# Attention's chunks in one list with a fixed order per engine, sums of x moved into the retention, loads of made products asked for ahead

## The chip, the cores and the metric

The kernel runs on one core of one Trainium2 chip. The metric is the device time of one execution in microseconds (us), given as the median of several runs. The core has five engines that run their own instruction streams in order: TensorE (PE, matmuls and transposes; its weight loads are listed apart as PEld), VectorE (DVE), ScalarE (ACT), GpSimd (POOL) and SyncE (SP), which here issues nearly all DMAs.

## The reference

One encoder layer. 16 learned meta tokens are put in front of x (1024 rows of 1024), so there are 1040 positions.

```
u = rms_norm(h, pre_w)
z = u @ w_in                       # 7680 columns
rq, rk, rv, rg, aq, ak, av, ag, gr, ga = split(z)
# branch A: 4 heads of bidirectional retention in chunks of 128, with decays
o_r = group_norm(retention_forward + retention_backward) * ret_nw * silu(rg)
# branch B: 8 query heads in 2 groups, windowed softmax attention, a sink logit, the meta keys always visible
s = rotary(aq) . rotary(ak) * scale + mask        # 128 queries, up to 384 + 16 keys
m = max(max(s), sink);  p = exp(s - m)
o_a = (p / (sum(p) + exp(sink - m))) @ v * silu(ag)
mix = sigmoid(gr) * (o_r @ w_rb) + sigmoid(ga) * (o_a @ w_ab)
out = h + rms_norm(mix @ w_out, post_w)
```

## The kernel before

All matmuls are in split float32: each operand is a high part h and a low part l in the fast format, and `mm3` (L69) adds three matmuls hh, lh, hl (lines L71, L72, L73) into one PSUM tile. High parts are made on ScalarE or GpSimd (`pool_hi`, L75), low parts on VectorE by subtraction (`dve_lo`, L78).

The work goes through these stages:

- **Start** (to about 46 us): x is loaded, split into `big`, and the queries and keys of retention head 0 are projected.
- **Retention** (`retention`, L434; to about 349 us). For each head h: a forward loop over c = 0..8, in which `stage1(c + 1)` projects a chunk of V (`pv`), splits it (L465, L466) and makes the decayed keys and scores, and `stage2(c)` forms the inner and cross products (`pa`) and the state (`pkv`); then a backward loop with `pb`, the group norm and transposes (`to`).
- **Attention** (`attention`, L1207; about 349 to 616 us). Called for four pairs of heads hp, each with 8 chunks n of 128 queries for two heads e_. `stage1(n)` makes the scores of both heads (`ps`, three matmuls each), the row minimum on VectorE (L1254), the exponential with its sum on ScalarE (L1257), the reciprocal (L1260) and the scaling on GpSimd (L1266). `stage2(n)` transposes the probabilities on PE (`pt`, L1276 to L1283) and splits them: pah and pal for the first two blocks of keys, pm for the meta keys, pbh and pbl for the third block. `stage3(n)` multiplies them with the values (`po`, seven or ten matmuls), copies the result to `oa` (L1312) and stores it every second chunk.
- **Gates and output projections** (`Phase`, `run`; from about 598 us): 16 pairs of weight blocks for the gates (`bz`), two branch projections and the output projection, by a seven-product scheme whose operands are sums and differences of quarter blocks.

Between the dependent steps of retention and attention stands independent work, the **filler**. `filler` (L604) joins generators; `fill(n)` advances them by n units. A unit of `gen_qk` (next retention head), `gen_ak` (attention keys) or `gen_aq` (attention queries, `paq`) is one step of the inner dimension, three matmuls; 8 units make one PSUM tile, which `rope_evac` (L158) rotates with three VectorE operations and one GpSimd addition. `gen_pre(u)` (L701) makes one or two of the gates' seven products ahead of their stage (**made products**, `pe`, 4 units each): it loads raw weights (`we`), forms a combination in three VectorE subtractions or additions (L711 to L713), splits it and stores the products to `e_d`. `FILL` (L26) says how many units follow each chunk of attention. The lists are `fills(hp)` (L1346).

`sum_row(k)` (L666) makes four rows of differences of x's quarter blocks for the later stage: two loads, two scalings on ScalarE (L672), four subtractions on VectorE (L676), four stores to `xs_d` (L677). It is called in attention, for hp 1 and 2 after chunks 2 and 5.

All raw weights, and the rows of `sum_row`, go through two SBUF buffers of 512 KB with the tag `wr`; the split weights through four buffers `wh` and four `wl`. A load can be issued when its buffer's last reader is done.

The order of every engine's instructions is set at build time: the tile context is opened with `schedule_with_timeline_sim=True`, and its planner orders the traced instructions by its own estimate of times, earlier traced ones first where several are ready. `with tc.issue_after(i):` puts each instruction of the block that runs on the engine of i behind i. Attention before has one such edge in its loop, which keeps the filler behind the third score product before the latest pair:

```
with tc.issue_after(scored[-5]) if len(scored) > 4 else ExitStack():
    fill(FILL[hp][n])
```

So what PE does between the scores, transposes and value products of neighbouring chunks is the planner's choice. `x_to_out` (L1340) copies most of x to out, DRAM to DRAM, behind the first store of attention.

Of the kernel before, what the change touches and what calls it, by code (L numbers as in the profile page):

```python
# [25 lines left out]
FILL = (6, 5, 5, 5, 5, 5, 5, 4), (6,) * 8, (6, 5, 5, 4, 4, 4, 4, 0), (7, 7, 7, 7, 6, 6, 8)  # L26
# [12 lines left out]
def block_kernel(ctx: ExitStack, tc: tile.TileContext, xT, x, w_in, w_rb, w_ab, w_out, vecs, dec, sink,  # L39
# [28 lines left out]

    def mm3(o, ah, al, bh, bl, first, last, free_group=False):  # L69
        kw = {"skip_group_check": True} if free_group else {}  # L70
        nc.tensor.matmul(o, ah, bh, start=first, stop=False, **kw)  # L71
        nc.tensor.matmul(o, al, bh, start=False, stop=False, **kw)  # L72
        return nc.tensor.matmul(o, ah, bl, start=False, stop=last, **kw).ins  # L73
# [360 lines left out]
    def retention(h, fill):  # L434
# [194 lines left out]

    def gen_aq(hp, i):  # L630
        if not i:
            wq[hp] = load_w(w_in, U_AQ + hp)
            aq[hp] = {}
        a, b = HALVES[i]
        for e_ in range(2):
# [3 lines left out]
            aq[hp][e_, i] = o  # L639
            yield  # L640
# [3 lines left out]

    def gen_ak(g):
        if not wak:
            wak.append(load_w(w_in, U_AK))
# [17 lines left out]

    def sum_row(k):  # L666

        x = {}
        for i in range(2):
            t = keep.tile([P, 4, 256], F32, tag="wr", bufs=2, name=f"xs{i}{k}").rearrange("p a b -> p (a b)")  # L670
            nc.sync.dma_start(t, xT[4 * i + k, :, NM:T])
# [3 lines left out]
        for n, o, a, b in SUMS:  # L675
            nc.vector.tensor_tensor(x[o], x[a], x[b], ALU.subtract)  # L676
            nc.sync.dma_start(xs_d[n][k], x[o])  # L677

# [22 lines left out]
    def gen_pre(u):  # L701

        g = nc.vector.tensor_tensor
        n = P * len(PRE[u])
        raw = [keep.tile([P, 4, 256], F32, tag="wr", bufs=2, name=f"we{u}_{j}") for j in range(len(PRE[u]))]
        for j, t in enumerate(reversed(raw)):
            nc.sync.dma_start(t[:, :, 0:n], w_in[gates[u], :, 4 - 4 * j:8 - 4 * j, 0:n])
        t = raw[-1]
        if n > P:
            v = t[:, :, P:n]  # L710
            g(v, raw[0][:, :, P:n], v, ALU.add)  # L711
            g(v, v, raw[0][:, :, 0:P], ALU.subtract)
            g(v, t[:, :, 0:P], v, ALU.subtract)  # L713
        h = wp.tile([P, 4, 256], R, tag="wh", bufs=4, name=f"weh{u}")[:, :, 0:n]
        l = wp.tile([P, 4, 256], R, tag="wl", bufs=4, name=f"wel{u}")[:, :, 0:n]
        nc.scalar.copy(h, t[:, :, 0:n])
        dve_lo(l, t[:, :, 0:n], h)
        for p in PRE[u]:
# [9 lines left out]
            nc.sync.dma_start(e_d[u, p], o)  # L728
            yield
# [10 lines left out]
    pre = all_pre()  # L740
# [449 lines left out]
    def gen_av():  # L1190
        w = load_w(w_in, U_AV)
        for c in range(9):
# [9 lines left out]
            if c % 2 == 0:  # L1202
                yield

    scored, softmax, stored, values = [], [], [], {}

    def attention(hp, fill):  # L1207
        g = hp // 2
        kh, kl = kT[g]
# [257 lines left out]
```

## Time and profile before

| what | value |
|---|---|
| median of 3 runs | 1107.57 us (1107.34 to 1107.73) |
| profiled execution | 1106.49 us, span from first to last instruction 1104.7 us |
| mean granted TensorE clock | 0.994 |
| attention, stretch 349.1 to 592 us | PE busy 227.08 of 242.90 us |
| largest wait of PE by one releaser | ps behind nm (L1254): 11.6 us in 16 waits |

A row of the groups reads: line, engine, operation, output <- inputs by the program's names, shapes, count, then busy time in us and mean ns of one, then the idle time of the engine before them and what ended it. "Busy" of PE includes modelled ends of pipelined matmuls, so two neighbours overlap: a matmul of 512 columns is shown as 0.39 us and the next starts 0.23 us after it. A row of the stretches reads: start:end, length, then busy time and number of instructions of PE, PEld, DVE, ACT, POOL, then the granted clock, the DMA engines' busy share and GB/s.

### The profile page before, as it was taken

How to read it: one execution, taken by the hardware profiler on the slowest of the kernel's cores; microseconds unless marked ns; L12 is line 12 of the kernel's file. 1: busy time of each engine (PE TensorE's matmuls, PEld its weight loads, DVE VectorE, ACT ScalarE, POOL GpSimd, SP SyncE). 2: the span in 40 equal slices, each digit the busy share in tenths (PEclk: the TensorE clock that was granted, in tenths of full speed). 3: DMA queues.
4: the chain of work that ended last, by engine and by line, in shares of the span. 5: the costliest groups of instructions: out<-in, count | busy, mean ns of one | idle time of the engine just before them, and what ended most of it. 6: DMA issues, size and time to landing. Idle time of an engine off the chain costs nothing.

```text
span 1104.7 us, 17067 instructions
## 1 busy us (share of the span) xinstructions
PE 1067.4 (97%) x5939; PEld 916.4 (83%) x5939; DVE 875.6 (79%) x1797; ACT 504.1 (46%) x1126; POOL 219.8 (20%) x276
## 2 busy tenths in 40 slices
PE   8999999999999989998998999999999999999997
PEld 7898999988989867986787788788888888787886
DVE  7897778868976866788646899999789889866765
ACT  7141432513414534645356744545456545433442
POOL 3234225143332423333220000000000000010032
PEclk9999999999999999999999999999999999999999
DMA  7121102122122545333224857899963765779463
GB/s 285 39 68 57 52 27 68 58 62 83 49 96 77 182 144 180 126 105 115 79 90 157 276 196 272 303 349 349 365 204 121 231 210 176 233 200 326 142 115 77
DMA packets 82902, 175.16 MB, mean 159 GB/s; under 512 B 8784, under 2 KB 22608, under 8 KB 82000
## 3 DMA queue, kind: packets, MB, share of 16 engines
q1 hardware_dynamic: 78928, 167.51, 44.5%
q0 software_dynamic: 3456, 6.29, 3.7%
q8 instruction: 46, 0.75, 0.3%
q14 instruction: 40, 0.33, 0.1%
q10 hardware_dynamic: 432, 0.28, 0.1%
HBM read 119.52 MB, written 57.67 MB: 160 GB/s over the span
## 4 chain that ended last, share of the span: by engine, by line
PE 73%; DVE 10%; DMA 9%; ACT 3%; issue 3%; POOL 1%; SPq 0%; DVEq 0%; POOLq 0%; ACTq 0%
PE bz L71 6%; PE bz L72 6%; PE bz L73 6%; PE pv L71 3%; PE pv L72 2%; PE pv L73 2%; PE br L72 2%; PE br L71 2%; PE br L73 2%; PE bo L72 2%; PE bo L71 2%; PE bo L73 2%; DMA we<-in_w_in_dram 2%; PE ba L72 2%; PE ba L73 2%
## 5 line engine op out<-in xcount | busy, mean ns | idle before, releaser
L1105 POOL DMA_DIRECT2D mx_d<-c1a x4 | 3.7, 917 | 400.8 <-DVE c1a L1096 400.8
L71 PE MATMUL bz<-T,lhz 128*128 128x512 f32 x192 | 75.6, 395 | 1.1 <-ACT u2z L887 1.1
L72 PE MATMUL bz<-T,llz 128*128 128x512 f32 x192 | 75.7, 394 | 0.0
L73 PE MATMUL bz<-T,lhz 128*128 128x512 f32 x192 | 75.6, 395 | 0.0
L71 PE MATMUL pv<-wh,big 128*128 128x256 f32 x256 | 73.9, 289 | 1.2 <-DVE m_qk L164 1.2
L72 PE MATMUL pv<-wh,big 128*128 128x256 f32 x256 | 73.7, 288 | 0.0
L73 PE MATMUL pv<-wl,big 128*128 128x256 f32 x256 | 73.4, 287 | 0.0
L72 PE MATMUL bz<-big,llz 128*128 128x512 f32 x176 | 69.6, 395 | 0.0
L73 PE MATMUL bz<-big,lhz 128*128 128x512 f32 x176 | 69.3, 394 | 0.0
L71 PE MATMUL bz<-big,lhz 128*128 128x512 f32 x176 | 69.3, 398 | 0.0
L1254 DVE CUSTOM_DVE_ANT_0 raw<-ps,mask,nsink 128x400 f32<-128x400 f32 (+1 forms) x64 | 37.9, 595 | 28.8 <-ACT p L1257 28.1
L1266 POOL TENSOR_SCALAR p<-p,den 128x400 f32<-128x400 f32 (+1 forms) x60 | 40.7, 692 | 94.2 <-DVE den L1260 72.1
L71 PE MATMUL paq<-big,wh 128*128 128x512 f32 x128 | 51.2, 400 | 0.0
L73 PE MATMUL paq<-big,wh 128*128 128x512 f32 x128 | 51.1, 399 | 0.0
L72 PE MATMUL paq<-big,wl 128*128 128x512 f32 x128 | 51.0, 398 | 0.0
L71 PEld LDWEIGHTS pv<-wh,big 128*128 128x128 f32 x256 | 49.0, 192 | 1.7 <-DVE m_qk L164 1.5
L72 PEld LDWEIGHTS pv<-wh,big 128*128 128x128 f32 x256 | 49.0, 191 | 0.2
L73 PEld LDWEIGHTS pv<-wl,big 128*128 128x128 f32 x256 | 49.0, 191 | 0.0
L1257 ACT ACTIVATE p<-raw,nm 128x401 f32<-128x401 f32 (+1 forms) x64 | 38.8, 607 | 16.7 <-PE pt L1283 6.4
L71 PEld LDWEIGHTS bz<-T,lhz 128*128 128x128 f32 x192 | 36.2, 188 | 10.3 <-ACT u2z L887 1.9
L73 PEld LDWEIGHTS bz<-T,lhz 128*128 128x128 f32 x192 | 36.2, 188 | 8.4
L72 PEld LDWEIGHTS bz<-T,llz 128*128 128x128 f32 x192 | 36.2, 188 | 8.4
(631 smaller groups left out, 3633.6 us busy)
## 6 DMA issues: line engine op xcount, KB each, us to landing
wrz<-in_w_in_dram SPq DMA_DIRECT2D x32, 512.0 KB, 6.0
wr<-in_w_in_dram SPq DMA_DIRECT2D x29, 512.0 KB, 3.7
e<-e SPq DMA_DIRECT2D x40, 256.0 KB, 3.9
we<-in_w_in_dram SPq DMA_DIRECT2D x16, 512.0 KB, 3.8
tg<-tg_d SPq DMA_DIRECT2D x32, 256.0 KB, 5.0
T<-preT SPq DMA_DIRECT2D x6, 1024.0 KB, 8.6
oTr_d<-ost SPq DMA_DIRECT2D x16, 256.0 KB, 2.1
xs<-in_xT_dram SPq DMA_DIRECT2D x8, 512.0 KB, 3.4
```

What stands on the lines that cost most here:

```text
L71: nc.tensor.matmul(o, ah, bh, start=first, stop=False, **kw)
L72: nc.tensor.matmul(o, al, bh, start=False, stop=False, **kw)
L73: return nc.tensor.matmul(o, ah, bl, start=False, stop=last, **kw).ins
L1105: nc.gpsimd.dma_start(d, to, accum_op=ALU.add)
L1254: nc.vector.tensor_tensor_reduce(raw[e_][:, 1:1 + wid], s[:, 0:wid], mask[:, mo:mo + wid], -SCALE, nsink[:, hd:hd + 1], ALU.add, ALU.min, ...
L1257: nc.scalar.activation(p[:, 0:1 + wid], raw[e_][:, 0:1 + wid], AF.Exp, scale=-1.0, bias=nm_[:, e_:e_ + 1], accum_out=den[:, e_:e_ + 1])
L1266: nc.gpsimd.tensor_scalar(pt[e_][:, 0:wid], pt[e_][:, 0:wid], den[:, e_:e_ + 1], 1.0, op0=ALU.mult, op1=ALU.mult)
```

## The change

Five things are changed.

1. The four calls of `attention(hp, fill)` become one generator over a list of 32 chunks (hp, n). The first chunk of the next pair is thereby traced ahead of the last chunk of the pair before, except for (2, 0), whose keys belong to the second group.
2. A helper `follow` puts a block behind several instructions. `latest` holds the last matmul or transpose traced. In the loop, PE's order is fixed: scores of the next chunk, transposes of this one, filler, value products of this one. ScalarE and VectorE parts of the next scores stand behind the last `oa` copy and the last low part (`lo`); those of the transposes stand behind the last exponential (`exp`) and reciprocal (`sum`). The last two chunks are left to the planner, as before.
3. The projection of attention's V (`gen_av`) stops before its last block; that block comes behind the scores of chunk (0, 0). The low and high parts of the attention queries are made when the tile is rotated, except for pair 0's first half.
4. `sum_row` is split: `sum_fetch(h)` issues the loads at step c = 1 of retention head h, and the scalings, subtractions and stores run at c = 3, behind that step's split of V. Attention has none of it.
5. Weights of attention's filler are loaded from hooks at given units of the generators ahead of their use, and `gen_pre` is split into `pre_fetch` (loads), `pre_parts` (combination and split, behind the last reciprocal) and the products. The filler amounts are distributed anew; one made product (8 units) moves from pair 1 to pair 2, and half of the second group's keys (16 units) to the end of pair 1. The total is the same.

```diff
-FILL = (6, 5, 5, 5, 5, 5, 5, 4), (6,) * 8, (6, 5, 5, 4, 4, 4, 4, 0), (7, 7, 7, 7, 6, 6, 8)
+FILL = (6, 5, 5, 5, 5, 5, 4, 5), (6, 5, 5, 6, 6, 6, 6, 16), (6, 5, 5, 5, 5, 5, 4, 5), (7, 7, 7, 7, 6, 6, 8)
...
+    def follow(*ins):
+        st = ExitStack()
+        for i in ins:
+            st.enter_context(tc.issue_after(i))
+        return st
...
@@ retention, loop over c
             if c == 1:
                 while pend:
                     pend.pop(0)()
+                sum_fetch(h)
+            if c == 3:
+                with follow(state["v"], state["vl"]):
+                    sum_row(h)
...
@@ gen_aq
         if not i:
-            wq[hp] = load_w(w_in, U_AQ + hp)
+            if hp not in wq:
+                load_aq(hp)
...
             aq[hp][e_, i] = o
+            if hp or i:
+                split_q(hp, e_, i)
             yield
...
+    def pre_fetch(u):
         n = P * len(PRE[u])
         raw = [keep.tile([P, 4, 256], F32, tag="wr", bufs=2, name=f"we{u}_{j}") for j in range(len(PRE[u]))]
         for j, t in enumerate(reversed(raw)):
             nc.sync.dma_start(t[:, :, 0:n], w_in[gates[u], :, 4 - 4 * j:8 - 4 * j, 0:n])
+        fetched_w[u] = raw
+    def pre_parts(u):
+        raw, n = fetched_w.pop(u), P * len(PRE[u])
         t = raw[-1]
+        with follow(*softmax[-1:]):
...
+    def gen_pre(u):
+        if u not in parts:
+            pre_fetch(u)
+            pre_parts(u)
+        h, l = parts.pop(u)
+        ahead = 9 < u < 13
+        if ahead:
+            pre_fetch(u + 1)
         for p in PRE[u]:
...
+            if ahead and p == 2:
+                pre_parts(u + 1)
             yield
...
@@ attention
-        stage1(0)
-        for n in range(NB):
-            if n < NB - 1:
-                stage1(n + 1)
...
-            stage2(n)
-            if hp < 3 or n < NB - 2:
-                with tc.issue_after(scored[-5]) if len(scored) > 4 else ExitStack():
-                    fill(FILL[hp][n])
-            if hp in (1, 2) and n in (2, 5):
-                sum_row(2 * hp - 2 + n // 3)
...
-            stage3(n)
+        chunks = [(hp, n) for hp in range(4) for n in range(NB)]
+        fill = filler(fills(0))[0]
+        av = gen_av()
+        next(av)
+        stage1(0, 0)
+        with follow(*latest):
+            next(av, None)
+        for (hp, n), follows in zip(chunks, chunks[1:] + [None]):
+            if follows and follows != (2, 0):
+                with follow(*latest, *marks("oa", "lo")):
+                    stage1(*follows)
...
+            with follow(*latest, *marks("exp", "sum")) if (hp, n) < (3, NB - 2) else ExitStack():
+                stage2(hp, n)
+            if (hp, n) < (3, NB - 2):
+                if (hp, n) == (1, NB - 1):
+                    fill = filler(fills(2))[0]
+                with follow(*latest):
                     fill(FILL[hp][n])
...
+            with follow(*latest) if (hp, n) < (3, NB - 2) else ExitStack():
+                stage3(hp, n)
+            if follows == (2, 0):
+                with follow(*latest, *marks("oa", "lo")):
+                    stage1(2, 0)
+                with follow(*latest):
+                    fill(2 * KT)
...
     def fills(hp):
-        l = [gen_aq(hp, 1), pieces(pre, (8, 16, 0, 32)[hp])]
-        if hp == 2:
-            l.insert(0, gen_ak(1))
-        if hp < 3:
-            l.append(gen_aq(hp + 1, 0))
-        return l
+        if hp == 1:
+            return [hooked(gen_aq(1, 1), {5: [(pre_fetch, 8)], 11: [(pre_parts, 8)], 15: [(load_aq, 2)]}), pieces(pre, 8),
+                    hooked(gen_aq(2, 0), {5: [(load_ak,)]})]
+        if hp == 3:
+            return [hooked(gen_aq(3, 1), {3: [(pre_fetch, 10)], 9: [(pre_parts, 10)]}), pre]
+        return [*([gen_ak(1)] if hp else []), hooked(gen_aq(hp, 1), {5: [(load_aq, hp + 1)]}),
+                hooked(gen_aq(hp + 1, 0), {3: [(pre_fetch, 7 + hp)], 9: [(pre_parts, 7 + hp)]}), pieces(pre, 8)]
```

More of the change, by code (lines that the diff above doesn't have):

```diff
@@ L72, in mm3 @@
         nc.tensor.matmul(o, al, bh, start=False, stop=False, **kw)
-        return nc.tensor.matmul(o, ah, bl, start=False, stop=last, **kw).ins
+        latest[:] = [nc.tensor.matmul(o, ah, bl, start=False, stop=last, **kw).ins]
+        return latest[0]
+    def follow(*ins):
[3 more added lines that the diff above has]
+        return st
     def pool_hi(o, i):
@@ L738, in all_pre @@
             yield from gen_pre(u)
-    pre = all_pre()
+    pre, fetched_w, parts = all_pre(), {}, {}
+    scored, softmax, stored, values = [], [], [], {}
     with tc.issue_after(normed):
@@ L1201, in gen_av, with attention, vsplit @@
                 nc.scalar.activation(vraw[:, c - 1], t[:, 0:256], AF.Copy, scale=rcol[:, c:c + 1])
-            if c % 2 == 0:
+            if c == NB - 1:
                 yield
[L1205 to L1209, printed above, removed]
-        kh, kl = (t.rearrange("p a b -> p (a b)") for t in (kh, kl))
-        vs = values.setdefault(g, {})
+    def attention():
         oa, raw = [None], {}
         st1, st2 = {}, {}
-        def vsplit(b):
+        def vsplit(hp, b):
+            g = hp // 2
             a_ = ap.tile([P, P], R, tag="vh", bufs=NB, name=f"vh{hp}_{b}")
@@ L1311, in stage3 @@
             o0 = P * (n % 2)
[L1312 removed]
+            last["oa"] = nc.scalar.copy(oa[0][:, :, o0:o0 + P],
+                                        po[:, 0:256].rearrange("p (e t) -> p e t", e=2)).ins
             if n % 2:
```

116 lines of the change are left out of this document (65 added, 51 removed).

## The prediction

> **What bounds the kernel now.** I read the page first, then the busy time by stretches, then the groups of the stretch that the change rewrites, then single moments of it.
>
> ```profile
> span 1104.7 us, 17067 instructions
> PE 1067.4 (97%) x5939; PEld 916.4 (83%) x5939; DVE 875.6 (79%) x1797; ACT 504.1 (46%) x1126; POOL 219.8 (20%) x276
> ```
>
> TensorE (PE) is busy in 97% of the span, so an edit pays only where PE waits. The stretches tell where that is (columns: PE, weight loads, VectorE, ScalarE, GpSimd busy with their instructions, then clock, DMA share, GB/s).
>
> ```profile
> 103.00:245.00 142.00, 142.00 (x1069) 134.56 (x1068) 113.23 (x289) 49.78 (x149) 47.73 (x69) 1.00 0.17 56
> 245.00:319.50 74.50, 71.97 (x523) 66.84 (x522) 62.16 (x158) 24.74 (x75) 25.87 (x34) 1.00 0.27 90
> 319.50:349.10 29.60, 29.14 (x246) 28.63 (x245) 19.52 (x58) 9.61 (x26) 9.40 (x16) 1.00 0.08 28
> 349.10:592.00 242.90, 227.08 (x1281) 193.53 (x1279) 168.99 (x392) 125.34 (x333) 74.18 (x86) 0.99 0.38 124
> 440.00:500.00 60.00, 60.00 (x380) 54.40 (x379) 45.88 (x109) 32.32 (x90) 21.94 (x25) 1.00 0.39 126
> 592.00:616.00 24.00, 21.73 (x107) 17.78 (x108) 20.26 (x37) 17.20 (x40) 0.00 (x0) 0.93 0.74 251
> 640.00:660.00 20.00, 20.00 (x88) 16.20 (x87) 19.15 (x33) 11.68 (x21) 0.00 (x0) 1.00 0.61 193
> ```
>
> Attention, 349.1 to 592, has 15.8 us without PE work (242.90 - 227.08). The retention before it has almost none until head 3 (245 to 319.5: 2.5 us), and the projection of V beside the end of head 3 (319.5 to 349.1) 0.5. Busy hides more, since a matmul's modelled end reaches past the next one's start. So I count the work of attention instead.
>
> ```profile
> L71 PE MATMUL paq<-big,wh 128*128 128x512 f32 x112 | 44.9, 401 | 0.0
> L71 PE MATMUL pe<-big,weh 128*128 128x512 f32 x56 | 22.1, 394 | 0.0
> L71 PE MATMUL ps<-kTh,aqh 128*128 128x400 f32 x48 | 18.5, 386 | 7.1 <-DVE nm L1254 7.1
> L71 PE MATMUL po<-pah,vh 128*128 128x256 f32 x58 | 17.6, 303 | 2.0 <-ACT oa L1312 2.0
> ```
>
> Each row stands for one of the three matmuls of a product. So 3 x (112 + 56) = 504 of the 1281 have 512 columns, 144 have 400, and 633 have 128 to 272. The spacing of 512 columns is 20.00 / 88 = 0.227 us (row 640:660). For the others I use 0.18 and, between the 0.11 of a transpose and the 0.125 of 272 columns, 0.117. That makes 114 + 26 + 74 = 214 us of work in 242.9: **about 28 us of attention is not work.** One such place:
>
> ```profile
> 392.01 0.28 PE L72 MATMUL po<-pah,vl 128*128 128x256 f32 x1
> 392.13 0.28 PE L73 MATMUL po<-pal,vh 128*128 128x256 f32 x1
> 393.34 0.39 PE L71 MATMUL po<-pbh,vh 128*128 128x256 f32 x1 [0.55 <-ACT pbh L1298]
> 395.23 0.49 PE L71 MATMUL ps<-kTh,aqh 128*128 128x272 f32 x1 [1.39 <-DVE nm L1254]
> 395.97 0.63 PE L71 MATMUL paq<-big,wh 128*128 128x512 f32 x1
> 396.39 0.63 PE L72 MATMUL paq<-big,wl 128*128 128x512 f32 x1
> ```
>
> The scores (ps) and the value products (po) of neighbouring chunks stand beside each other with no filler (paq) between. Each waits for a softmax or split only just started, and the filler comes when nothing waits. Between 440 and 500 the filler lies between them and PE has no idle time at all: the same chunk, better ordered, is free of waits.
>
> The rows at 395.97 and 396.39 start 0.42 us apart where warm ones start 0.227 apart: after waits of 0.55 and 1.39 us PE runs at about half rate. [...]
>
> **The change, part by part.** *Fixed order in the chunk loop.* PE's order becomes scores of chunk n+1 (S), transposes of n (T), filler, value products of n (O). PE works on S for 6 x 0.18 = 1.1 us, on T for 8 x 0.11 = 0.9, on 5 filler units for 15 x 0.227 = 3.4, on O for 10 x 0.117 = 1.2: 6.6 us. The chains that must fit:
>
> ```profile
> L1254 DVE CUSTOM_DVE_ANT_0 raw<-ps,mask,nsink 128x400 f32<-128x400 f32 x48 | 30.0, 629 | 17.7 <-ACT p L1257 17.1 <-PE ps L73 0.3
> L1257 ACT ACTIVATE p<-raw,nm 128x401 f32<-128x401 f32 x48 | 30.4, 633 | 9.8 <-PE pt L1279 3.8 <-PE pt L1283 2.7 <-DVE nm L1254 2.6
> L1257 ACT ACTIVATION_READ_ACCUMULATOR p<-raw,nm 128x1 f32 x64 | 12.1, 188 | 0.0
> L1266 POOL TENSOR_SCALAR p<-p,den 128x400 f32<-128x400 f32 x46 | 32.2, 714 | 76.6 <-DVE den L1260 54.6 <-PE pt L1279 15.0 <-PE pt L1276 6.4
> L1286 ACT CAST pah<-pt 128x512 fp32r<-128x512 f32 x32 | 18.5, 577 | 8.8 <-PE pt L1276 8.7
> L79 DVE TENSOR_TENSOR pal<-pt,pah 128x512 fp32r<-128x512 f32 x32 | 22.0, 687 | 7.8 <-ACT pah L1286 7.5
> L79 DVE TENSOR_TENSOR pm<-pt,pm 16x256 fp32r<-16x256 f32 x32 | 13.3, 415 | 4.6 <-ACT pm L1290 3.5
> L79 DVE TENSOR_TENSOR pbl<-pt,pbh 128x256 fp32r<-128x256 f32 x24 | 9.9, 415 | 0.0
> ```
>
> Count from the start of S, with 0.1 us per hand-over (an estimate). The first score block ends at 0.7, its row minimum at 1.4. The two exponentials, 0.63 + 0.19 each, end at 3.1. ScalarE may only then cast T's result (3.7), and VectorE subtracts it: pal 4.5, pm 4.9, pbl 5.3. O starts at 1.1 + 0.9 + 3.4 = 5.4, needs pal at its third matmul and pbl near its ninth: about 1 us of slack. The other chain goes on from 3.1 over the reciprocal and two GpSimd scalings (1.4) to 4.9; T of n+1 starts at 6.6 + 1.1 = 7.7: nearly 3 us of slack. VectorE also has floating work from the filler:
>
> ```profile
> L162 DVE TENSOR_TENSOR m_aq<-paq,cr 128x512 f32<-128x512 f32 x16 | 11.0, 687 | 2.6 <-PE paq L73 2.4
> L79 DVE TENSOR_TENSOR aql<-aq,aqh 128x512 fp32r<-128x512 f32 x16 | 11.9, 750 | 3.6 <-ACT aqh L625 3.5
> ```
>
> per 8 units three rotary products (2.06) and one split (0.75), 1.8 us per chunk of 5 units, on top of about 3 us of the chunk itself. So VectorE is some 75% full, and a floating piece ahead of pal uses up most of that slack, but rarely more. For the waits that stay I take 0.2 us per chunk, 31 x 0.2 = 6, nearest to row 440:500, which has 0; the other bound is 0.9 per chunk, where everything stays as it is. So of 28 us, **22 go** (bounds 0 and 28).
>
> *Loads asked for ahead, and no sums in attention.* Now the two raw-weight buffers (tag wr) carry the sums of x between weights:
>
> ```profile
> 374.59 2.51 DMA xsT<-xs
> 386.61 11.75 DMA we<-in_w_in_dram
> ```
>
> A made product's load waited for the sums' stores, then took 11.75 us beside the copy of x to out, and the filler behind it was late at 398. The change takes the sums out and asks earlier: 10 to 12 filler units ahead of the first use, two chunks of 6.6 us or 13 us against the 11.75 of this worst load; in the last pair of heads 8 units ahead, 8 x 3 x 0.227 = 5.4 us of filler plus the chunk's own work. That work hides the load, its issue on SyncE, and the casts. The copy itself stays, since its condition, the first stored output, is the same. If that cover goes, PE, now in fixed order, stands still for the rest of a load. I count the gain within the 22, as the idle time is the same idle time; a moved load by itself costs nothing.
>
> *Start of attention.* Filler now comes only behind T of chunk 0, and V's last block (24 matmuls, 2.8 us) behind the first scores. These need the splits of the queries:
>
> ```profile
> 350.07 1.14 ACT L625 CAST aqh<-aq 128x512 fp32r<-128x512 f32 x2
> 352.74 1.29 DVE L79 TENSOR_TENSOR aql<-aq,aqh 128x512 fp32r<-128x512 f32 x2
> ```
>
> PE's other work ends at 349.1 - 2.8 = 346.3. If the casts can start only when the retention's buffers are free (they came right behind its last output here), scores start at about 350.7 even when VectorE takes the split first: 4.4 us idle, 0.5 of them idle already. If they may start earlier, nothing. I take **3 lost** (0 to 4.5), nearer to the row.
>
> *Sums in the retention.* Per head this adds on SyncE two loads at step 1 and four stores at step 3, on ScalarE two scalings, on VectorE four subtractions:
>
> ```profile
> L672 ACT ACTIVATE xs<-xs,vec 128x1024 f32<-128x1024 f32 x8 | 9.2, 1152 | 11.5 <-DMA xs<-in_xT_dram 10.5 <-DMA xsT<-xs 0.9 <-DVE pbl L79 0.2
> L676 DVE TENSOR_TENSOR xs<-xs 128x512 f32<-128x512 f32 x8 | 5.7, 710 | 5.7 <-ACT xs L672 5.7
> wr<-in_w_in_dram SPq DMA_DIRECT2D x29, 512.0 KB, 3.7
> L76 POOL TENSOR_SCALAR wh<-wr 128x1024 fp32r<-128x1024 f32 x26 | 29.4, 1132 | 32.0 <-PE pv L72 8.8 <-DMA wr<-in_w_in_dram 5.5 <-PE pav L72 4.2
> L79 DVE TENSOR_TENSOR wl<-wr,wh 128x1024 fp32r<-128x1024 f32 x28 | 35.0, 1257 | 5.9 <-POOL wh L76 5.7
> 126.53 0.37 ACT L465 CAST vh<-pv 128x256 fp32r<-128x256 f32 x1
> 137.53 0.37 PE L71 MATMUL pk<-big,wh 128*128 128x272 f32 x1
> ```
>
> That is 2.3 us on ScalarE and 2.8 on VectorE, ahead of the chunk's own chain. VectorE is 80% and (head 3) 83% busy in the rows 103:245 and 245:319.5. PE covers 2 or 3 us of delay where it has filler; head 3 idles already. The sums also hold both wr buffers until stored, and the next head's query and key weights queue behind them on SyncE, with that head's output stores behind those. In head 1 the gate is the fifth V block, 126.5; sums to about 133, stores 2.5, load 3.7, cast 1.1 and split 1.3: 141.5 instead of 137.5 for the first key filler. PE would lack up to 4 us of filler, and without it idles perhaps a third of that. I take 1 us per head, **4 in all**, nearest to the fully busy row 103:245; the bounds are 0 and 4 x (2.8 + 1.3) = 16.
>
> *Sum.* -22 + 3 + 4 = -15. The profiled execution took 1106.49 (span 1104.7 and 1.8 around it), 1.1 below the median 1107.57. Its 1091.5 corresponds to a median of about **1093**. The end of attention, 592:616 (2.3 idle), keeps its code and its waits.
>
> **The rivals.** *The retention gives it back* (sums late, filler late, VectorE full): 12 instead of 4 us, so 1101; for it speak head 3's 2.5 us of idle time, against it the 142.00 of 142.00. Chance 0.15. *It doesn't do what it says:* the late load was the cause and not the order; then only some 10 us around 391 to 440 and 500 to 535 go, and the rest of attention keeps its waits: 1107.6 - 10 + 7 = 1104. Against it: the waits named are on nm, oa and pbh, not on weights. Chance 0.08. *Slower:* floating VectorE work goes ahead of pal in every chunk that has it. The 2.06 + 0.75 us less 1.0 of slack is 1.8 us of PE wait, in 5 of 8 of 32 chunks: 36 us that PE, bound to its order, can't fill. 1107.6 - 28 + 36 + 7 = 1122. It decides from 21 / 31 = 0.7 us per chunk; against it speaks that the chunk's own instructions can be put first. Chance 0.12.
>
> **How the numbers follow.** The forecast has 0.65. Its own bounds run from 1081 (attention free of waits, start and retention nearly free) to 1101. The range up to 1107 takes in the two rivals that are still faster and leaves out the slower one and a few in a hundred at either end. A measurement of this kernel tells about 0.2% (2.2 us) from no change. Faster by more: 0.65 + 0.13 + 0.05 = 0.83; within: 0.05; slower: 0.12.
>
> **What would show it.** In attention PE idles under 7 us and runs S, T, filler, O in blocks. The wait of the 400-column ps on nm shrinks from 7.1 us to under 2; the made products' first operation (L711) no longer waits for its load. At the start of attention a gap of 3 to 4 us stands ahead of the first ps. In the retention pk starts some 3 us later per head, with little idle time. If instead each O waits for pal, or the filler of a head starts far later, the forecast is wrong.

## The result, and the profile after

The changed kernel takes 1137.87 us (median of 4 runs, 1132.23 to 1143.39) against 1107.65 for the kernel before on the same chip: ratio 1.027 [1.0218, 1.0321]. It is **slower by 2.7%**, where 1093 was forecast and 1107 was the upper end of the range. The profiled execution took 1137.18 us, its span is 1135.3, 30.6 more than before. From the page of the changed kernel:

```profile
span 1135.3 us, 17083 instructions
PE 1080.5 (95%) x5939; PEld 926.6 (82%) x5939; DVE 881.0 (78%) x1797; ACT 507.1 (45%) x1126; POOL 216.4 (19%) x276
```

The instructions are nearly the same (16 more in 17,000, none of them a matmul), so the 30.6 us are waits and slow clock. The stretches that the prediction showed, in the changed kernel (two heads of retention, head 3, the projection of V, attention, a piece of its middle, and the first 13 us of attention):

```profile
106.00:256.10 150.10, 144.21 (x1051) 134.52 (x1050) 116.06 (x298) 52.19 (x152) 48.32 (x71) 0.99 0.25 80
256.10:335.00 78.90, 75.28 (x537) 69.86 (x536) 66.04 (x161) 27.17 (x77) 25.83 (x35) 0.98 0.32 106
335.00:358.90 23.90, 23.90 (x205) 23.85 (x204) 16.11 (x50) 6.86 (x18) 7.70 (x13) 1.00 0.07 23
358.90:624.10 265.20, 236.99 (x1313) 204.22 (x1312) 170.39 (x389) 126.14 (x339) 72.25 (x87) 0.95 0.25 83
440.00:500.00 60.00, 54.18 (x309) 47.19 (x309) 39.87 (x82) 25.80 (x71) 20.25 (x21) 0.91 0.23 76
358.90:372.00 13.10, 8.17 (x40) 7.01 (x39) 6.60 (x21) 5.21 (x17) 2.76 (x5) 0.74 0.13 42
```

The retention, which had PE busy 142.00 of 142.00 us before, now has 5.9 us without PE work in two heads. Attention has 28.2 (265.20 - 236.99) instead of 15.8, and its clock is 0.95: a clock of 0.95 over 265.20 us is some 13 us lost (an estimate: 0.05 of the stretch). The stretch 440 to 500, free of waits before, has 5.8 us idle and 0.91.

Two landmarks give a clean account, since the work ahead of them and between them is the same in every kernel here but for the sums of x, which are what is moved: the first matmul with the backward state in head 3 of the retention (`pb`) and the first gate product behind attention (`bz`). The timeline of the kernel before, then of the changed one:

```profile
321.94 0.36 PE L71 MATMUL pb<-Shb,qh 128*128 128x256 f32 x1 [0.34 <-DVE op L509]
598.25 0.77 PE L71 MATMUL bz<-big,lhz 128*128 128x512 f32 x1
```

```profile
338.20 0.28 PE L73 MATMUL pb<-Shb,qh 128*128 128x256 f32 x1
630.28 0.47 PE L73 MATMUL bz<-big,lhz 128*128 128x512 f32 x1
```

- Up to `pb` (call it the retention): 321.9, now 338.2: **+16.3**.
- From `pb` to `bz` (call it attention, V's projection included): 276.3, now 292.1: **+15.8**.
- From `bz` to the end of the span: 506.5, now 505.0: -1.5.

These are stretches of one execution each. The changed kernel and e3, e4 and e5 below run the same work ahead of `pb`, almost instruction for instruction, and have it at 338.2, 334.6, 337.0 and 338.4. So a difference of less than 4 us between two such stretches can be chance.

**What PE waits for in attention.** The order is the one that the change asks for: S, T, filler and O in blocks. The waits of the 400-column scores on nm are gone. New ones stand in their place (the list of PE's waits in the changed kernel; us in total, times, longest):

```profile
PE po L75 <- DVE pbl L89: 9.9, 6, 2.2
PE ps L73 <- ACT aqh L639: 8.7, 4, 2.5
PE po L73 <- ACT pbh L1353: 3.3, 5, 0.9
PE ps L74 <- DVE aql L89: 2.8, 3, 1.7
```

One of the scores' four waits on aqh is at attention's start; the others are one place in each of the first three pairs of heads. The timeline of the changed kernel at the fifth chunk of the first pair, PE, VectorE, GpSimd and ScalarE:

```profile
391.65 0.39 PE L75 MATMUL paq<-big,wh 128*128 128x512 f32 x1
391.88 0.28 PE L73 MATMUL po<-pah,vh 128*128 128x256 f32 x1
392.08 0.69 DVE L172 TENSOR_TENSOR m_aq<-paq,cr 128x512 f32<-128x512 f32 x1
392.79 0.69 DVE L173 TENSOR_TENSOR m_aq<-paq,sr 64x512 f32<-64x512 f32 x1
393.43 0.34 PE L75 MATMUL ps<-kTl,aqh 128*128 128x400 f32 x1
393.48 0.69 DVE L174 TENSOR_TENSOR m_aq<-paq,sr 64x512 f32<-64x512 f32 x1
394.26 1.26 POOL L175 TENSOR_TENSOR aq<-m_aq,m_aq 128x512 f32<-128x512 f32 x1 [3.12 <-DVE m_aq L174]
395.56 0.62 ACT L639 CAST aqh<-aq 128x512 fp32r<-128x512 f32 x1
396.21 0.69 DVE L89 TENSOR_TENSOR aql<-aq,aqh 128x512 fp32r<-128x512 f32 x1 [0.53 <-ACT aqh L639]
396.23 0.45 PE L73 MATMUL ps<-kTh,aqh 128*128 128x400 f32 x1 [2.46 <-ACT aqh L639]
```

Chunks 4 to 7 read the second half of the pair's queries. Its 16 filler units are spread 6, 5, 5 over chunks 0, 1 and 2, so its last product (391.65) comes out just ahead of O(2) and S(4). Behind it stand three rotary products, GpSimd's addition, a cast and a split: 4.8 us from 392.08 to 396.9, and PE's fixed order has only O(2) and the first head's three score products, 1.9 us together (391.88 to 393.77), to cover them.

The other new wait, of po on pbl, is VectorE's order (timeline of the changed kernel, one chunk of the second pair):

```profile
443.76 0.68 DVE L172 TENSOR_TENSOR m_aq<-paq,cr 128x512 f32<-128x512 f32 x1
444.45 0.69 DVE L173 TENSOR_TENSOR m_aq<-paq,sr 64x512 f32<-64x512 f32 x1
445.15 0.69 DVE L174 TENSOR_TENSOR m_aq<-paq,sr 64x512 f32<-64x512 f32 x1
445.88 0.41 DVE L89 TENSOR_TENSOR pm<-pt,pm 16x256 fp32r<-16x256 f32 x1
446.73 0.42 DVE L89 TENSOR_TENSOR pbl<-pt,pbh 128x256 fp32r<-128x256 f32 x1 [0.44 <-ACT pbh L1353]
446.75 0.38 PE L73 MATMUL po<-pbh,vh 128*128 128x256 f32 x1 [0.61 <-ACT pbh L1353]
```

The three rotary products of the filler stand ahead of pm and pbl, 2.06 us: the mechanism of the rival that was called slower.

**The retention.** The weights of the next head are late, as the groups of the changed kernel show (the row of the casts on GpSimd, by far the most of its wait now on the load, where before 5.5 of 32.0 us were), and as the timeline shows for head 1, changed kernel first, then the kernel before:

```profile
L86 POOL TENSOR_SCALAR wh<-wr 128x1024 fp32r<-128x1024 f32 x26 | 29.2, 1126 | 43.0 <-DMA wr<-in_w_in_dram 38.7 <-PE pt L1337 1.7 <-PE pq L75 1.5
```

```profile
131.01 0.89 DVE L704 TENSOR_TENSOR xs<-xs 128x512 f32<-128x512 f32 x1
134.93 0.68 DVE L704 TENSOR_TENSOR xs<-xs 128x512 f32<-128x512 f32 x1
139.92 1.05 POOL L86 TENSOR_SCALAR wh<-wr 128x1024 fp32r<-128x1024 f32 x1 [4.04 <-DMA wr<-in_w_in_dram]
```

```profile
137.41 1.05 POOL L76 TENSOR_SCALAR wh<-wr 128x1024 fp32r<-128x1024 f32 x1 [5.33 <-PE pv L72]
```

The four subtractions lie between the chunk's own instructions from 131.01 to 135.6, the buffers come free after their stores, and the cast waits 4.04 us for the load, where it waited for PE before. The first key product of head 1 moved from 137.5 to 142.7, that of head 2 from 207.9 to 216.9.

### The profile page after: what moved, and what is told of

Same layout as the page of the kernel before. It is cut to its first block, busy times and chain, and to the rows that moved or that the text cites. A ratio compares the mean times of both kernels' runs of the same rounds, so it can differ in the third digit from the quotient of the medians.

```text
span 1135.3 us, 17083 instructions
## 1 busy us (share of the span) xinstructions
PE 1080.5 (95%) x5939; PEld 926.6 (82%) x5939; DVE 881.0 (78%) x1797; ACT 507.1 (45%) x1126; POOL 216.4 (19%) x276
## 4 chain that ended last, share of the span: by engine, by line
PE 74%; DVE 12%; DMA 7%; issue 3%; ACT 3%; POOL 1%; SPq 0%; DVEq 0%; POOLq 0%; ACTq 0%
PE bz L73 6%; PE bz L74 6%; PE bz L75 6%; PE pv L73 2%; PE br L74 2%; PE br L75 2%; PE br L73 2%; PE pv L74 2%; PE pv L75 2%; PE bo L73 2%; PE bo L74 2%; PE bo L75 2%; PE ba L74 2%; PE ba L73 2%; PE ba L75 2%
## 5 line engine op out<-in xcount | busy, mean ns | idle before, releaser
L1320 POOL TENSOR_SCALAR p<-p,den 128x400 f32<-128x400 f32 (+1 forms) x60 | 38.4, 654 | 130.4 <-DVE den L1313 113.4
L89 DVE TENSOR_TENSOR wl<-wr,wh 128x1024 fp32r<-128x1024 f32 x28 | 37.3, 1335 | 15.3 <-POOL wh L86 15.1
```

The costliest lines, as they stand in the source:

```text
L89: return nc.vector.tensor_tensor(o, i, hi.bitcast(F32), ALU.subtract).ins
L1320: nc.gpsimd.tensor_scalar(pt[e_][:, 0:wid], pt[e_][:, 0:wid], den[:, e_:e_ + 1], 1.0, op0=ALU.mult, op1=ALU.mult)
```

## The experiments

Three questions: whether the retention's 16.3 us are the sums and by what; whether attention's loss is the fixed order or some late producers in it; and what the sums cost where they were. The texts on record call the theories by letters and say in each place what they are.

**e1: the changed kernel with the sums back in attention.**

```
-                sum_fetch(h)
-            if c == 3:
-                with follow(state["v"], state["vl"]):
-                    sum_row(h)
...
                     fill(FILL[hp][n])
+                if hp in (1, 2) and n in (2, 5):
+                    sum_fetch(2 * hp - 2 + n // 3)
+                    sum_row(2 * hp - 2 + n // 3)
```

> The changed kernel with the sums of x taken out of the retention and made in attention again, at the places they had before (after chunks 2 and 5 of pairs 1 and 2); nothing else differs. Theory A (the sums cost the retention about 17 us: the first backward product of head 3 came 16 us later in the changed kernel): the retention returns to its old length, that product comes at about 322 us, and the time falls by 10 to 17 us, to 1121 to 1128, less what the sums cost in attention. Rival B (the retention got longer because the planner, seeing other work behind it, ordered it otherwise): it comes no earlier than 335 us and the time stays at 1135 or more.

1135.75 us, ratio 1.0247 [1.0222, 1.0272]. `pb` is at 319.8, 18.4 earlier: the retention's loss is the sums. But from `pb` to `bz` it takes 308.0 instead of 292.1: in the fixed order the sums cost 16 us in attention as well, so nothing is won.

**e2: the kernel before, with the sums in the retention alone.**

```
+                sum_fetch(h)
+            if c == 3:
+                with follow(state["v"], state["vl"]):
+                    sum_row(h)
...
-            if hp in (1, 2) and n in (2, 5):
-                sum_row(2 * hp - 2 + n // 3)
```

> The kernel before with one part of the change alone: the sums of x fetched at step 1 and made at step 3 of each retention head, none in attention. Theory A: the retention gets 12 to 17 us longer (first backward product of head 3 at 334 to 338 us), attention gets a few us shorter without the sums, the time is 1115 to 1124. Rival B: the retention stays within 3 us of the old length and the time is 1102 to 1109.

1113.47 us, ratio 1.0049 [1.0033, 1.0064], 1.5 below theory A's range. `pb` is at 335.8 (+13.9), as that theory said, and attention takes 266.6, **9.7 less than before, with the old order**. Against this kernel the rest of the change adds 25.5 us to attention (292.1).

**e3: the changed kernel with the filler as one stream over all pairs, 5 units ahead**, so that the second half of the queries ends a chunk earlier.

```
-FILL = (6, 5, 5, 5, 5, 5, 4, 5), ...
+FILL = (11, 5, 5, 5, 5, 5, 4, 5), ...
...
-        fill = filler(fills(0))[0]
+        fill = filler([g for k in range(4) for g in fills(k)])[0]
```

> The changed kernel with the filler as one stream that runs 5 units ahead (11 units instead of 6 behind the first chunk), so that the second half of a pair's queries is finished one chunk earlier and not right ahead of the scores of chunk 4 that read it. Theory A (PE waits there because the rotation, the GpSimd addition and the split of that half, about 5 us, have only the value products of 1.2 us to hide behind, and the slow clock after it costs 1.7 us more): the waits of ps on aqh and aql, 11.5 us in all, fall under 4 us, two to four slow clock phases go, and the time falls by 10 to 18 us, to 1120 to 1128. Rival B (VectorE is the limit in these chunks, and the wait moves to the value products): the waits of po grow by as much, and the time falls by less than 5 us.

1125.7 us, ratio 1.0161 [1.0134, 1.0189]: 12 us less, as theory A said. In the profiled executions 9.9 of them are attention's (292.1 to 282.2) and 3.6 stand ahead of `pb`, where the edit changes nothing. The waits of ps on the queries fall from 11.5 to 3.3 us, and these two are at attention's start:

```profile
PE ps L74 <- DVE aql L89: 1.7, 1, 1.7
PE ps L73 <- ACT aqh L639: 1.6, 1, 1.6
```

**e4: the changed kernel with the filler's VectorE and ScalarE work behind the chunk's splits.**

```
-                with follow(*latest):
+                with follow(*latest, *marks("hi", "lo")):
                     fill(FILL[hp][n])
```

> The changed kernel with one more edge: the filler's VectorE and ScalarE instructions of a chunk stand behind that chunk's own last split (pbl) and last cast (pbh). Theory A (rotary products, weight splits and made products' combinations get ahead of pal and pbl, and PE's value products wait): the waits of po on pbl, pal and pbh, 14.6 us in all, fall under 4 us, and with the slow clock phases they cause the time falls by 10 to 18 us, to 1120 to 1128. Rival B (the work pushed back is late next: the query halves and weights come later): the waits of ps on aqh and aql grow from 11.5 us by as much, and the time stays at 1133 to 1143.

1140.31 us, ratio 1.0291 [1.0261, 1.032]: nothing gained. The waits of po shrink from 14.6 to 2.5 us, and those of ps take their place, since the queries are now later still:

```profile
PE ps L73 <- ACT aqh L639: 17.9, 7, 3.6
PE ps L74 <- DVE aql L89: 3.6, 4, 1.7
PE po L75 <- DVE pbl L89: 1.6, 2, 0.8
```

**e5: e3 and e4 together.**

> The changed kernel with both earlier edits: filler stream 5 units ahead, and the filler's VectorE and ScalarE instructions behind the chunk's own splits. Theory A (the two waits are one resource: whichever goes first on VectorE, the other is late; only with a chunk of lead for the query halves can the splits go first at no cost): the waits of po on pbl, pal and pbh stay under 4 us, those of ps on aqh and aql under 5, and the time is 1110 to 1119. Rival B (the lead of one chunk isn't enough, since the pushed-back work accumulates): ps on aqh and aql is 8 us or more, the time 1122 to 1130.

1128.17 us, ratio 1.0186 [1.0155, 1.0217]. The waits are as theory A said and the total is as rival B said, for a reason that neither names: both waits are small, and a third comes up: the made products' weights, whose combinations on VectorE were pushed back with the rest.

```profile
PE pe L73 <- ACT weh L751: 10.6, 3, 5.0
```

**e6: e2 without the sums' arithmetic**: the kernel before, with the sums' loads and stores alone in the retention.

```
-            nc.scalar.activation(t, t, AF.Copy, scale=vec[:, 4 * i + k:4 * i + k + 1])
...
-            nc.vector.tensor_tensor(x[o], x[a], x[b], ALU.subtract)
```

> The kernel before with the sums alone in the retention, but without their scalings and subtractions: the rows of x are loaded into the weight buffers and stored as they are at the same places, so the later stage reads other data. Theory A (the retention gets longer because the rows hold both weight buffers until the fifth V block of the head, and the next head's key weights come late): the first backward product of head 3 stays at 331 us or later, as with the sums (335.8), and the time is 1108 to 1114. Rival B (the 2.3 us on ScalarE and 2.8 us on VectorE per head delay the forward loop): that product comes at 322 to 327, and the time is 1100 to 1106.

1093.31 us, ratio 0.9879 [0.9849, 0.9909], below both ranges. `pb` at 322.0, attention 264.3. Without the arithmetic nothing is left for the gate at step 3 to hold back, so the rows were stored as soon as they had landed and the buffers were not held either. It takes away both suspects and can't tell them apart. What it shows is what the sums cost beyond their loads and stores: with the old order, some 13 us.

**e7: the kernel before, each head's sums without a gate, behind the load of V's weights of the next head.**

```
         wv = wv0 if h == 0 else load_w(w_in, U_V + h)
+        if h:
+            sum_fetch(h - 1)
+            sum_row(h - 1)
```

> The kernel before with the sums in the retention at another place: row k is fetched and made right behind the load of V of head k + 1 (the last row behind the load of attention's V), without the gate on the fifth V block, so it runs beside the backward loop of head k, when both weight buffers otherwise hold the next head's weights waiting. Theory A (holding the weight buffers in the forward loop is the cost): the retention is back within 3 us of the old length (first backward product of head 3 at 319 to 325), attention keeps its gain of about 7 us, the time is 1099 to 1104, faster than before. Rival B (the arithmetic costs wherever it stands): head 3's product comes at 330 or later, the time is 1107 to 1114.

1108.01 us, ratio 0.9997 [0.9974, 1.0019]. `pb` is 5.6 late instead of 13.9, between the two theories, and attention takes 268.8. The loads out of the way of the weights recover more than half of the retention's loss.

**e8: e5 with the sums placed as in e7.**

> The changed kernel with the stream 5 units ahead, the filler's work behind the splits, and the sums beside the backward loops. Theory A: as e5, less the 14 to 16 us that the sums cost in the retention: 1095 to 1105. Rival B: the sums cost there what they cost in the forward loop: 1108 to 1119, as e5.

1122.23 us, ratio 1.0125 [1.0093, 1.0158], above both ranges: against e5 the retention gives back 7.1 us (`pb` 338.4 to 331.3), but attention takes 285.7 (283.9 in e5) and keeps the wait on weh.

**e9: e2 with the sums' arithmetic on one or two columns**, the gate and the held buffers kept.

```
-            nc.scalar.activation(t, t, AF.Copy, scale=...)
+            nc.scalar.activation(t[:, 0:513:512], t[:, 0:513:512], AF.Copy, scale=...)
...
-            nc.vector.tensor_tensor(x[o], x[a], x[b], ALU.subtract)
+            nc.vector.tensor_tensor(x[o][:, 0:1], x[a][:, 0:1], x[b][:, 0:1], ALU.subtract)
```

> The kernel before with the sums in the retention, as in the earlier run of them alone, but the two scalings work on two columns and the four subtractions on one column (the sums that are stored are therefore not the reference's): the gate, the two raw-weight buffers held until the stores and the order on SyncE stay, the arithmetic of 2.3 us on ScalarE and 2.8 us on VectorE per head nearly goes. Theory H (the buffers held make the next head's weights late): the retention keeps at least two thirds of its +14 us, first scores at 363 or later, total 1109 to 1113. Theory A (the arithmetic ahead of the retention's own chain on VectorE and ScalarE): first scores at 354 to 357, total 1094 to 1099.

1102.25 us, ratio 0.9954 [0.994, 0.9968], between the two theories: `pb` at 328.0 (+6.1; e2 +13.9). So with next to no arithmetic the held buffers cost 6.1. The other 7.8 come with the arithmetic, and not only because it stands ahead of the retention's own work: it also keeps the buffers longer. The first load of weights behind the stores of head 1's sums is issued 4 us earlier in e9 than in e2, and GpSimd's casts wait 23.6 us for loads against 34.5 (first e9's rows, then e2's):

```profile
129.59 0.33 SPq L103 DMA_DIRECT2D wr<-in_w_in_dram  x1
L83 POOL TENSOR_SCALAR wh<-wr 128x1024 fp32r<-128x1024 f32 x26 | 29.1, 1118 | 32.1 <-DMA wr<-in_w_in_dram 23.6 <-PE pa L72 3.4 <-PE pq L73 1.5
```

```profile
133.82 0.43 SPq L103 DMA_DIRECT2D wr<-in_w_in_dram  x1
L83 POOL TENSOR_SCALAR wh<-wr 128x1024 fp32r<-128x1024 f32 x26 | 29.1, 1118 | 40.8 <-DMA wr<-in_w_in_dram 34.5 <-PE pav L72 1.5 <-PE pq L73 1.4
```

**e10: e7 with the subtractions on GpSimd; e11: the scalings there too.**

```
-            nc.vector.tensor_tensor(x[o], x[a], x[b], ALU.subtract)
+            nc.gpsimd.tensor_tensor(x[o], x[a], x[b], ALU.subtract)
```

> The kernel before with the sums made early in the retention (1108.01 with the subtractions on VectorE, first scores 7.4 us late), and the four subtractions of a head on GpSimd. If VectorE's 2.8 us per head are the price, first scores are at most 3 us late and the total is 1100 to 1104. If the held buffers are the price, GpSimd holds them longer (at least 1.3 us per subtraction instead of 0.7), the first scores are 7 to 12 us late and the total is 1108 to 1113.

1102.74 us, ratio 0.9962 [0.994, 0.9984]: **below both kernels**. The total is in the range of the theory that VectorE's 2.8 us per head are the price, but not for its reason: `pb` is as late as in e7 (328.0) and the first scores 6.9 us late. What makes it faster than e7 isn't shown, and since the two intervals overlap, it isn't certain that it is faster. Attention is 3.7 us shorter (265.1 instead of 268.8), but behind `bz` e10 loses 3.0 again: the two profiled spans are 1102.8 and 1103.1 us.

> As the run with the subtractions on GpSimd, and the two scalings of a head on GpSimd too, so that VectorE and ScalarE do none of the sums. If the arithmetic is the price, 1097 to 1102. If the held buffers are, or if GpSimd's own casts of the weights now queue behind some 9 us of sums per head, 1109 to 1116 with the wait of pk on wh grown above 5 us.

1105.92 us, ratio 0.9979 [0.9964, 0.9994]: above the one theory's range and below the other's. `pb` at 326.1, attention 268.9. Its interval overlaps that of e10, so the scalings' place decides nothing that these runs can tell.

**e12: e8 with the made products' weights fetched and combined 2 to 5 filler units earlier.**

```
-  {5: [(pre_fetch, 8)], 11: [(pre_parts, 8)], 15: [(load_aq, 2)]}
+  {0: [(pre_fetch, 8)], 6: [(pre_parts, 8)], 11: [(load_aq, 2)]}
...
-  {3: [(pre_fetch, 10)], 9: [(pre_parts, 10)]}
+  {1: [(pre_fetch, 10)], 7: [(pre_parts, 10)]}
```

In the last pair each further weight is fetched as soon as the one before it is combined.

> The fixed order with all three corrections (1122.2), and the made products' weights fetched and made 3 to 4 filler units earlier: PE waited 10.6 us for weh there, in three places. Theory: each wait of the fixed order has its own late producer and goes when that producer is put earlier; then the wait on weh falls under 3 us, and with the slow clock behind it the total is 1107 to 1112, no better than before the change. Rival: VectorE has no room in attention for the floating work wherever it is put; then the waits of po on pal and pbl or of ps on aql grow by what weh gives up, and the total is 1117 to 1122.

1108.42 us, ratio 1.0009 [0.9991, 1.0026]: by the ratios, each to the kernel before on its own chip, some 13 us less than e8, and level with the kernel before. The wait on weh fell without any other growing by as much:

```profile
PE po L75 <- DVE pbl L89: 2.7, 4, 0.8
PE po L75 <- DVE pal L89: 2.1, 5, 0.6
PE pe L73 <- ACT weh L750: 1.2, 1, 1.2
```

**e13: e12 without the rule of e4.** This asks whether the floating work ahead of the splits costs anything by itself.

> The fixed order with its late producers put right (1108.4), but without the rule that the filler's VectorE and ScalarE work of a chunk comes behind that chunk's splits. Theory V (the floating work ahead of the splits costs PE by itself): the waits of po on pbl, pbh and pal go back from some 5 us to 13 us or more, with the slow clock behind it 1115 to 1121. Theory Q (they were only a sign of a VectorE that ran late behind queries and weights): the waits stay under 7 us and the total is 1105 to 1110.

1117.83 us, ratio 1.0085 [1.006, 1.0109]: 9 us more than e12, in theory V's range. The waits of po come back, though less than that theory said (11.2 us in all with 1.3 on pm and 1.0 on pbh; 13 or more expected), and the clock is lower as well (0.984 against 0.991):

```profile
PE po L75 <- DVE pbl L89: 6.3, 4, 2.1
PE po L75 <- DVE pal L89: 2.6, 4, 1.1
```

**e14: e12 with the subtractions on GpSimd.**

> The fixed order with its late producers put right (1108.4), and the sums' subtractions on GpSimd, as the floating order had them at 1102.7. If the order of the chunks is worth nothing by itself, the same 4 us come off: 1103 to 1106, no better than the floating order with the same sums. If the fixed order has a gain of its own once VectorE is relieved, below 1100.

1110.1 us, ratio 1.0017 [1.0, 1.0034]. The fixed order shows no gain of its own, and the 4 us that both theories counted on did not come: attention takes 273.7, as in e12 (273.5).

The stretches of the profiled executions together (us; `pb` and `bz` read as above):

| kernel | up to pb | pb to bz | ratio |
|---|---|---|---|
| before | 321.9 | 276.3 | 1 |
| changed | 338.2 | 292.1 | 1.0270 |
| e1 sums back in attention | 319.8 | 308.0 | 1.0247 |
| e2 old order, sums in the retention | 335.8 | 266.6 | 1.0049 |
| e7 old order, sums early | 327.6 | 268.8 | 0.9997 |
| e10 as e7, subtractions on GpSimd | 328.0 | 265.1 | 0.9962 |
| e6 old order, no arithmetic | 322.0 | 264.3 | 0.9879 |
| e3 queries early | 334.6 | 282.2 | 1.0161 |
| e8 three corrections | 331.3 | 285.7 | 1.0125 |
| e12 all corrections | 328.7 | 273.5 | 1.0009 |
| e13 as e12, floating work first | 330.4 | 281.9 | 1.0085 |

## Why the prediction was wrong

**Step "fixed order" (-22): failed, in sign.** It named some 28 us of attention as not work and gave 22 of them to the order of the chunks, loads and sums counted within. The runs show otherwise:

- Some 8 to 12 belonged to the sums of x. Taken out with the order left alone, attention fell from 276.3 to 266.6 (e2), 268.8 (e7) and 264.3 (e6). The prediction saw the sums hold up the load at 386.61 and still gave their removal no term of its own in attention; it put it inside the 22. Of the rival "the late load was the cause and not the order" that half was right, though the runs don't show whether it is the load or the arithmetic that costs in attention.
- No run shows a gain of the order itself. With the same sums, and every late producer that was found put right, the fixed order takes 273.5 and the floating one 268.8 (e12 and e7), with totals that are level; with the subtractions on GpSimd 273.7 and 265.1 (e14 and e10), and there the total of the fixed order is the longer one. As written, the change adds 25.5 us to attention (292.1 against e2's 266.6).
- The other 16 to 20 us stayed in every kernel here; whose they are is open.

Three producers are late in it, each shown by a run that puts it right. The second half of the queries, with 1.9 us of cover for 4.8 us of chain: 9.9 us of attention (e3). The made products' weights, once the filler's work stands behind the splits: 12.2 (e8 to e12, at its worst 5.0 us in one wait). The floating VectorE work ahead of pm, pal and pbl: 8.4 (e13 against e12). They don't add up singly, since putting one right pushes another back (e4, e5). The prediction's count of the chunk followed the softmax and the splits alone; the queries' chain, which it quoted by its prices (2.06 and 0.75 us), was never laid against the place of its first use. That it is the fixed order which turns such a lateness into a wait is argued from the lists of waits: the kernel before has none on the queries or on weh, since its planner could put filler there.

**Step "loads asked for ahead" (0 by itself): right for the loads, wrong for what follows them.** VectorE's first combination waits 2.1 us for its loads in attention instead of 5.5. What came late once the filler's work was put behind the splits is the cast and the three combinations behind a load that has landed (e5).

**Step "start of attention" (3 lost, 0 to 4.5): right in kind, too small.** The changed kernel's first scores:

```profile
363.24 0.91 PE L73 MATMUL ps<-kTh,aqh 128*128 128x272 f32 x2 [1.62 <-ACT aqh L639]
365.83 0.59 PE L74 MATMUL ps<-kTh,aql 128*128 128x272 f32 x1 [1.68 <-DVE aql L89]
```

That is 3.3 us of waits, and the clock of 0.74 over 13.1 us (row 358.90:372.00) is 3.4 more: 6.7. The row has 4.9 us without PE work in all; the rest are mostly waits of the retention's last transposes, which other work of PE covered before. In the corrected order this is nearly all that is left against the floating one: counted by the spacing of matmuls as in the prediction (an estimate), e12 loses some 7 us from the last transposes to the second chunk's scores and e7 some 3, while all of attention differs by 4.7. No term of the prediction's sum stands for the clock, which was 0.50 from 364.2 to 371.0 (row 364.20:371.00 in the last section), with the wait of 1.62 us just ahead of that stretch and the wait of 1.68 us at its start.

**Step "sums in the retention" (+4): mechanism right, size wrong.** 16.3 us measured, just over the bound of 16. Late weights were named, and head 1's first key product came at 142.7 where 141.5 was worked out. The allowance that PE would idle for "perhaps a third" of the lateness failed: head 2's came 9.0 us late, and the delays of the heads added up to `pb` instead of being covered. e9 divides e2's 13.9: 6.1 by the held buffers alone, the rest with the arithmetic, which also holds them longer. The row 103:245, in which PE never idles, was taken as room. It says that PE has work all the time, and not that this work could be done in another order while its weights are late.

**The rivals.** The slower one, floating VectorE work ahead of the splits, had the right sign, and its mechanism is in the trace and worth 8 to 9 us in the corrected order (e13); it is not the whole, and its 1122 was short by 16. "The retention gives it back" was right in its mechanism, at 16 instead of 12; its 1101 was not, since it kept the 22. Each rival was priced as if it came alone; here two came together with a third that no part of the prediction named (the queries). The order S, T, filler, O, the vanished waits on nm and the gap at attention's start came as stated under what would show it. Idle time in attention under 7 us did not: 28.2.

**What stays open.** Whose the rest of the 28 us is; whether e10 differs from e7 and from e11 by more than chance, and by what; and which of the late producers costs how much alone, since they cover one another.

## What to carry to other kernels

Before an engine's order is fixed by hand, list for every block of it what it reads and the latest place at which that is made, over all engines: here one operand, late by some 3 us in one block of eight, went with 9.9 us of attention, and the kernel before, whose order floats, has no wait on it. Idle time in a stretch is not the order's until the same stretch has been seen without its foreign work; here the sums held some 10 of the 28 us, and no run shows that the order held any. The version that the runs point to keeps the old order, makes the sums early beside the loads of V's weights and subtracts on GpSimd: 1102.74 us, ratio 0.9962 [0.994, 0.9984] to the kernel before. That is a gain of 0.4%, small beside the 1.3% that the forecast promised.

## What the runs showed of the hardware

Read in stretches of 0.5 us, the granted clock of the changed kernel is 1.00 or 0.50, with other values only where a stretch holds a change from one to the other. Some longer stretches of its attention, then two of the kernel before:

```profile
358.90:364.20 5.30, 2.00 (x10) 0.94 (x8) 2.17 (x8) 3.86 (x12) 0.58 (x1) 1.00 0.29 99
364.20:371.00 6.80, 5.17 (x23) 5.07 (x24) 3.43 (x13) 1.22 (x4) 1.98 (x3) 0.50 0.01 4
396.20:405.00 8.80, 8.49 (x51) 7.41 (x52) 4.32 (x11) 3.37 (x10) 1.18 (x2) 1.00 0.07 22
409.50:412.00 2.50, 0.33 (x3) 0.32 (x3) 2.05 (x4) 0.79 (x1) 1.47 (x1) 1.00 0.44 175
412.00:415.40 3.40, 3.40 (x15) 3.11 (x14) 3.11 (x7) 2.21 (x7) 0.31 (x1) 0.50 0.22 48
415.50:420.00 4.50, 4.50 (x26) 3.84 (x25) 1.70 (x4) 1.95 (x6) 1.19 (x2) 1.00 0.18 67
```

```profile
395.40:398.70 3.30, 3.30 (x10) 2.72 (x11) 1.03 (x3) 0.62 (x1) 1.40 (x3) 0.50 0.41 129
398.80:405.00 6.20, 5.37 (x32) 4.23 (x31) 4.86 (x12) 3.93 (x10) 0.29 (x1) 1.00 0.49 137
```

In the changed kernel's attention (358.90 to 624.10) the clock is 0.50 five times, for 6.8, 3.4, 10.2, 3.4 and 3.4 us, 27.3 us in all. Half of that is some 13 us, as estimated above. The 28.2 us without PE work stand beside it, and no single wait on the list of PE's waits there is longer than 2.5 us. The kernel before has it at 0.50 once between 349 and 592, from 395.3 to 398.8; half of these 3.4 us is the 1.7 us that the text on record of e3 puts on a slow clock.

The longer of two waits was not the one with the slow clock behind it: behind the 2.46 us at 396.23 the clock stays at 1.00 to 405, and behind a wait of po on pbl of 2.17 us at 411.68 it is 0.50 from 412.0 to 415.4.

The four runs of the changed kernel spread over 11 us with mean clocks of 0.982, 0.987, 0.976 and 0.981; less the share lost to the clock they are 1116.7, 1117.5, 1116.0 and 1117.0 us. So all but 1.5 us of their spread goes with the clock, and by the same estimate some 14 of the 30 us between the two kernels are slow clock: the kernel before, at 0.994, comes to 1101.
